# Memory attention of the prompt in split fp32r operands: three one-pass matmuls in place of each two-pass fp32 matmul

## The chip, the cores and the metric

The kernel runs on one core of one Trainium2 chip. Its time is the device time of one execution in microseconds (us). A profile is one execution recorded by the hardware profiler. TensorE is PE in the rows (PEld its weight loads), VectorE is DVE, ScalarE is ACT, GpSimd is POOL, and SP issues nearly all DMAs, in order.

## What is computed

A decoder step of two layers over 512 prompt tokens and 8 x 8 sample tokens. Each layer ends with cross-attention into 256 memory tokens (four heads of 256) and a gated feed-forward network. The cross-attention, from the reference:

```python
def mem_attend(h, k, v, w_q, w_o):
    B, T, _ = h.shape
    q = (h @ w_q).reshape(B, T, MEM_HEADS, MEM_HEAD_DIM)
    s = jnp.einsum('bthe,bnhe->bhtn', q, k, preferred_element_type=F32) * MEM_HEAD_DIM ** -0.5
    p = jax.nn.softmax(s, axis=-1)
    o = jnp.einsum('bhtn,bnhe->bthe', p, v.astype(F32)).reshape(B, T, D_MODEL).astype(h.dtype)
    return o @ w_o
```

For the prompt, k and v are projected from the memory tokens in the kernel; for the sample they are read from a cache, 256 KB for each sequence, head and side.

## The kernel before

Activations stand transposed, channels on partitions and the 576 tokens along the columns, in two halves: 256 prompt tokens, and 256 prompt tokens with the 64 of the sample. A projection (`dense`) takes a weight of 128x1024 (`wr`), splits it on ScalarE into a high part in fp32r (`wh`, a cast) and on VectorE into the rest (`wl`, a subtraction), and makes each product of three one-pass matmuls: high by high, high by rest, rest by high. A matmul of plain fp32 operands runs in two passes, and the trace has two records for it.

A memory-attention stage (`mem_stage`, once in each layer) is written out by `sched`, a scheduler that works with fixed numbers at build time: every generator yields how much TensorE work it has just issued and how long to stay away, and the scheduler picks who issues next. Its filler is the projection of Q. Its lanes are two chains of `mem_prompt` (one for each half, four heads each), one chain of `mem_sample` (four heads, two blocks of four sequences), and the output projection, which waits for heads that are done.

- `mem_prompt(l, h, hf, ...)`: four matmuls for the scores of 256 tokens with 256 memory tokens; maximum on VectorE; exponential on ScalarE; division on VectorE; four transposes of the probabilities on TensorE, a copy on ScalarE; four matmuls with V; then the result is split into `oh` and `ol` for the output projection.
- `mem_sample(l, h, blk, ...)`: takes four K loads from the stream, eight small matmuls for the scores (32x256 in the rows), softmax, two transposes, takes four V loads, eight matmuls with V.

The loads of the sample's K and V come from `_Stream`. It issues a load into columns that the arena gives out, at the place in the program where `get` or `fill` is called; it loads ahead, up to eight, only while there is room:

```python
    def fill(self, n):
        while self.srcs and len(self.q) < n and self.prog.room() >= self.reserve + 512:
            self.load()
...
        return TOTAL - self.G * sum(int(p.taken.sum()) if p.dt == F32 else len(p.taken) for p in self.pages
                                    if p.taken.any())
```

The second piece is the arena's `room`: of 41472 columns it takes off the used ones of fp32 pages, and whole pages where they hold fp32r. The reserve here is `MROOM`, 4500. A load waits on SP until the last reader of its columns is done, and every DMA behind it on SP waits with it. All engines' instructions are recorded at one line (L630), so tiles tell them apart: `page` is the arena, `in_cmk` and `in_cmv` are the cached K and V, `in_w` the weights, `p` PSUM.

Of the kernel before, what the change touches and what calls it, by code (L numbers as in the profile page):

```python
# [9 lines left out]
F32R = mybir.dt.float32r  # L10
# [691 lines left out]
class _Prog:  # L702
# [1188 lines left out]
    def mem_stage(self, l, nx):  # L1891
        nc = self.nc
        Q = self.wide("mq", dt=F32)
        oh, ol = self.wide("xh"), self.wide("xl")
        done = set()

        def ev(i, hf, ps):
            t0, N = HALF[hf]
            nx.upto(hf)
            nc.vector.tensor_tensor(Q[i][:, t0:t0 + N], ps[:, :N], nx.R[:, t0:t0 + N], op=OP.mult)  # L1900
            done.add((i, hf))
            if len(done) == 2 * KT:
                nx.clear()

        q = lambda: self.dense(self.pos[f"mq{l}"], 8, KT, nx.h, nx.l, ev, first=6)

        fin = set()
        st = _Stream(self, [s for h in range(4) for k in range(2) for s in self.mem_src(l, h, k)], "Kb", 8, MROOM)
        lanes = [self.chain(*[self.mem_prompt(l, h, hf, Q, done, oh, ol, fin) for h in range(4)]) for hf in range(2)]
        lanes.append(self.chain(*[self.mem_sample(l, h, b, Q, done, st, oh, ol, fin) for h in range(4) for b in range(2)]))  # L1910
        nn = _Next(self, "g_ffn", l * 8)
        ready = lambda k: lambda: sum((k // 2, j) in fin for j in ("a0", "a1", "s0", "s1")) == 4

        def o():
            yield 0, 0, lambda: len(done) == 2 * KT
            yield from self.dense(self.pos[f"mo{l}"], 8, KT, oh, ol, self.res_evac(nn), first=6, ready=ready)

        f = self.sched(lanes + [o()], q(), METM)
        assert f is None or next(f, None) is None
        self.Kc[l], self.Vc[l] = None, None  # L1920
        return nn
# [2 lines left out]
        b = range(blk * 4, blk * 4 + 4)  # L1924
        return [self.aps["cmk"][l, i, h] for i in b] + [self.aps["cmv"][l, i, h] for i in b]

    def mem_prompt(self, l, h, hf, Q, done, oh, ol, fin):
        nc = self.nc
        yield 0, 0, lambda: (2 * h, hf) in done and (2 * h + 1, hf) in done and self.Vc.get(l) is not None and len(self.Vc[l]) == 4
        K, V = self.Kc[l], self.Vc[l]  # L1930
        mx, den = self.T([128, 2], "mx"), self.T([128, 2], "den")
        ps = self.PS()
        for tt in range(2):
            t = slice(hf * 256 + tt * 128, hf * 256 + tt * 128 + 128)
            for eh in range(2):
                nc.tensor.matmul(ps[:, tt * 256:tt * 256 + 256], Q[2 * h + eh][:, t], K[h][:, eh * 256:eh * 256 + 256],
                                 start=eh == 0, stop=eh == 1)
        nc.vector.tensor_reduce(mx[:], ps[:].rearrange("p (h n) -> p h n", h=2), axis=AX.X, op=OP.max)
        nc.vector.tensor_scalar(mx[:], mx[:], -1.0 / 16, None, op0=OP.mult)
        yield 1.7, 1.2  # L1940
        p_ = self.S([128, 512], s="P")
        for tt in range(2):
            c = slice(tt * 256, tt * 256 + 256)
            nc.scalar.activation(p_[:, c], ps[:, c], AF.Exp, bias=mx[:, tt:tt + 1], scale=1.0 / 16,
                                 accum_out=den[:, tt:tt + 1])
        del ps
        yield 0, 1.2
        nc.vector.reciprocal(den[:], den[:])
        for tt in range(2):
            c = slice(tt * 256, tt * 256 + 256)  # L1950
            nc.vector.tensor_scalar(p_[:, c], p_[:, c], den[:, tt:tt + 1], None, op0=OP.mult)
        yield 0, 1.2
        ps = self.PS()
        for tt in range(2):
            for kt in range(2):
                nc.tensor.transpose(ps[:, kt * 256 + tt * 128:kt * 256 + tt * 128 + 128],
                                    p_[:, tt * 256 + kt * 128:tt * 256 + kt * 128 + 128], self.ident)
        pt = self.S([128, 512], s="PT")
        nc.scalar.copy(pt[:], ps[:])
        del p_  # L1960
        yield 0.44, 1.5
        ps = self.PS()
        for vh in range(2):
            for kt in range(2):
                c = (h % 2) * 256 + vh * 128
                nc.tensor.matmul(ps[:, vh * 256:vh * 256 + 256], V[kt, h // 2][:, c:c + 128],
                                 pt[:, kt * 256:kt * 256 + 256], start=kt == 0, stop=kt == 1)
        d = slice(hf * 256, hf * 256 + 256)
        for vh in range(2):
            self.split(ps[:, vh * 256:vh * 256 + 256], oh[2 * h + vh][:, d], ol[2 * h + vh][:, d])  # L1970
        fin.add((h, f"a{hf}"))
        yield 1.7, 0

    def mem_sample(self, l, h, blk, Q, done, st, oh, ol, fin):

# [529 lines left out]
```

## Time and profile before

| | us |
|---|---|
| three runs: median (lowest to highest) | 2044.92 (2040.68 to 2045.32) |
| the profiled execution: its time | 2044.57 |
| its span, first to last instruction | 2042.4 |
| PE busy, share of the span | 1987.4, 97% |
| DVE, ACT, POOL busy | 1252.5, 798.2, 264.2 |
| stage of layer 0: from 398 to 563, PE busy | 162.19 of 165 |
| stage of layer 1: from 1428 to 1592, PE busy | 159.97 of 164 |

Busy time is the time in which an engine had an instruction under way. Matmuls are pipelined, so a matmul's own length is more than its share of the engine; what a matmul costs is read from the start of one row to the start of the next. "Idle before" tells how long an engine stood still ahead of a row, and the name behind the arrow what ended it.

### The profile page before, as it was taken

What the parts mean: (1) busy time and instruction counts of PE and PEld (TensorE: products, weight loads), DVE (VectorE), ACT (ScalarE), POOL (GpSimd) and SP (SyncE); (2) the same over time, 40 slices, a digit from 0 to 9 for tenths busy, and PEclk for the clock granted to TensorE, in tenths of its full rate; (3) what the DMA queues carried; (4) which work ended last, traced back from release to release, by engine and by line L of the source; (5) the groups of instructions that cost most, each with busy time, mean ns of one, the idle gap of its engine ahead of it and who ended that gap; (6) DMA issues with size and microseconds to landing.
All of it is one profiled execution on the core that took longest, in us unless ns stands there. A gap on an engine that the chain in (4) does not pass through costs nothing.

```text
span 2042.4 us, 40671 instructions
## 1 busy us (share of the span) xinstructions
PE 1987.4 (97%) x16443; PEld 1849.4 (91%) x16443; DVE 1252.5 (61%) x3020; ACT 798.2 (39%) x1674; POOL 264.2 (13%) x570
## 2 busy tenths in 40 slices
PE   6999999999999999999999999999999999999997
PEld 6899877978999999999899888879779999999996
DVE  7686676644577467467516676656545675575575
ACT  5564424333444234234322442455334442342342
POOL 1133121000012012011003222200000021121111
PEclk9999999999999999999999999999999999999998
DMA  4221235555322222222554565675553222222222
GB/s 149 73 66 52 76 114 191 169 188 193 108 66 91 84 82 83 83 83 78 167 165 157 196 203 177 220 246 175 171 196 109 80 83 94 74 83 90 76 72 76
DMA packets 104091, 252.29 MB, mean 124 GB/s; under 512 B 11168, under 2 KB 22048, under 8 KB 103904
## 3 DMA queue, kind: packets, MB, share of 16 engines
q1 hardware_dynamic: 103760, 249.49, 37.8%
q8 instruction: 129, 2.11, 0.4%
q14 instruction: 58, 0.48, 0.1%
q10 hardware_dynamic: 144, 0.22, 0.0%
HBM read 227.70 MB, written 21.96 MB: 122 GB/s over the span
## 4 chain that ended last, share of the span: by engine, by line
PE 87%; DVE 6%; ACT 3%; DMA 3%; issue 1%; POOL 0%; SPq 0%; DVEq 0%; ACTq 0%; POOLq 0%
PE p L630 87%; DVE page L630 4%; ACT page L630 2%; DVE wl L630 1%; DMA wr<-in_w 1%; ACT wh L630 1%; DVE rn L630 1%; DMA page<-in_cmk 1%; DMA out_o_ss<-page 0%; DMA page<-xd 0%; DMA page<-in_x 0%; POOL page L630 0%; ACT L630 0%; SPq L630 0%; DMA xd<-page 0%
## 5 line engine op out<-in xcount | busy, mean ns | idle before, releaser
L630 PE MATMUL p<-page,wh 128*128 128x256 f32 (+1 forms) x7296 | 1101.9, 299 | 18.0 <-ACT wh L630 12.8
L630 PEld LDWEIGHTS p<-page,wh 128*128 128x128 f32 x7296 | 1013.2, 191 | 51.2 <-issue 25.8
L630 PE MATMUL p<-page,wl 128*128 128x256 f32 (+1 forms) x3648 | 589.8, 298 | 0.0
L630 PEld LDWEIGHTS p<-page,wl 128*128 128x128 f32 x3648 | 519.8, 191 | 8.2 <-issue 7.2
L630 DVE TENSOR_TENSOR page<-p,page 128x256 f32<-128x256 f32 (+5 forms) x647 | 241.8, 392 | 322.1 <-PE p L630 235.5
L630 ACT CAST wh<-wr 128x1024 fp32r<-128x1024 f32 (+1 forms) x268 | 274.6, 1028 | 378.2 <-PE p L630 297.4
L630 DVE TENSOR_TENSOR wl<-wr,wh 128x1024 fp32r<-128x1024 f32 (+1 forms) x268 | 332.9, 1245 | 83.2 <-ACT wh L630 76.4
L630 DVE SCALAR_TENSOR_TENSOR page<-page,vecs,page 128x256 f32<-128x256 f32 (+4 forms) x545 | 283.8, 526 | 97.5 <-ACT page L630 86.6
L630 PE MATMUL p<-page,page 64*64 64x64 f32 (+13 forms) x3768 | 280.7, 297 | 10.6 <-DVE page L630 4.0
L630 ACT ACTIVATE page<-page,vecs 128x256 f32<-128x256 f32 (+5 forms) x319 | 168.6, 537 | 231.9 <-DVE page L630 226.0
L630 PEld LDWEIGHTS p<-page,page 64*64 64x64 f32 (+6 forms) x3768 | 184.0, 130 | 69.5 <-issue 20.7
L630 POOL COPY page<-page 128x16 f32<-128x16 f32 (+5 forms) x312 | 128.5, 436 | 732.4 <-DVE page L630 732.4
L630 ACT ACTIVATE page<-page 128x256 f32<-128x256 f32 (+6 forms) x293 | 115.8, 410 | 139.1 <-DVE page L630 132.8
L630 POOL TENSOR_TENSOR page<-page,page 128x320 f32<-128x320 f32 (+6 forms) x96 | 91.7, 963 | 446.1 <-DVE page L630 321.8
L630 ACT COPY page<-p 128x256 f32<-128x256 f32 (+8 forms) x161 | 62.5, 413 | 162.4 <-PE p L630 159.9
L630 PE MATMUL p<-wh,page 128*128 128x512 f32 (+1 forms) x368 | 119.1, 397 | 0.0
L630 DVE TENSOR_TENSOR page<-page,page 128x256 fp32r<-128x256 f32 (+8 forms) x181 | 81.5, 463 | 57.4 <-ACT page L630 56.4
L630 DVE TENSOR_TENSOR page<-page 128x256 f32<-128x256 f32 (+5 forms) x222 | 97.9, 454 | 14.6 <-POOL page L630 9.4
L630 ACT CAST page<-page 128x256 fp32r<-128x256 f32 (+2 forms) x118 | 50.1, 439 | 126.0 <-DVE page L630 126.0
L630 PEld LDWEIGHTS p<-wh,page 128*128 128x128 f32 (+1 forms) x368 | 77.3, 223 | 14.5 <-issue 2.5
L630 PE MATMUL p<-cid,page 128*128 128x128 f32 (+3 forms) x669 | 78.3, 258 | 5.6 <-ACT page L630 4.0
L630 POOL MEMSET page<- 128x2 f32 (+4 forms) x110 | 12.2, 111 | 530.6 <-PE p L630 281.8
(84 smaller groups left out, 808.3 us busy)
## 6 DMA issues: line engine op xcount, KB each, us to landing
wr<-in_w SPq DMA_DIRECT2D x252, 512.0 KB, 3.6
page<-in_ck SPq DMA_DIRECT2D x72, 256.0 KB, 5.1
page<-in_cv SPq DMA_DIRECT2D x72, 256.0 KB, 4.4
page<-in_cmk SPq DMA_DIRECT2D x64, 256.0 KB, 5.0
page<-in_cmv SPq DMA_DIRECT2D x64, 256.0 KB, 4.8
wr<-in_w SPq DMA_DIRECT2D x16, 384.0 KB, 3.1
xd<-page SPq DMA_DIRECT2D x16, 288.0 KB, 4.3
out_o_v<-page SPq DMA_DIRECT2D x12, 256.0 KB, 4.5
```

Of the source, the lines that this page charges most:

```text
L630: return f(*args, **kw)
```

## The change

In `mem_prompt`, K, Q, the transposed probabilities and V are each split into a high part and a rest in fp32r, by `split` (a cast on ScalarE, a subtraction on VectorE), and each two-pass matmul becomes three one-pass ones. Parts of K and V of a head are made once and kept in `parts` until the second half of the prompt has used them; those of Q and of the probabilities are made in each call. A new yield of 1.5 stands between the split of Q and the scores, and two yields that stand for matmul work are 1.44 in place of 1.7. The copy of the transposed probabilities becomes the cast of their split. The whole diff:

```diff
@@ -1904,9 +1904,9 @@
 
         q = lambda: self.dense(self.pos[f"mq{l}"], 8, KT, nx.h, nx.l, ev, first=6)
 
-        fin = set()
+        fin, parts = set(), {}
         st = _Stream(self, [s for h in range(4) for k in range(2) for s in self.mem_src(l, h, k)], "Kb", 8, MROOM)
-        lanes = [self.chain(*[self.mem_prompt(l, h, hf, Q, done, oh, ol, fin) for h in range(4)]) for hf in range(2)]
+        lanes = [self.chain(*[self.mem_prompt(l, h, hf, Q, done, parts, oh, ol, fin) for h in range(4)]) for hf in range(2)]
         lanes.append(self.chain(*[self.mem_sample(l, h, b, Q, done, st, oh, ol, fin) for h in range(4) for b in range(2)]))
         nn = _Next(self, "g_ffn", l * 8)
         ready = lambda k: lambda: sum((k // 2, j) in fin for j in ("a0", "a1", "s0", "s1")) == 4
@@ -1924,20 +1924,37 @@
         b = range(blk * 4, blk * 4 + 4)
         return [self.aps["cmk"][l, i, h] for i in b] + [self.aps["cmv"][l, i, h] for i in b]
 
-    def mem_prompt(self, l, h, hf, Q, done, oh, ol, fin):
+    def mem_prompt(self, l, h, hf, Q, done, parts, oh, ol, fin):
         nc = self.nc
         yield 0, 0, lambda: (2 * h, hf) in done and (2 * h + 1, hf) in done and self.Vc.get(l) is not None and len(self.Vc[l]) == 4
-        K, V = self.Kc[l], self.Vc[l]
+        V = self.Vc[l]
         mx, den = self.T([128, 2], "mx"), self.T([128, 2], "den")
+        two = lambda s: [self.S([128, 512], F32R, s=s) for _ in range(2)]
+        if ("k", h) not in parts:
+            kh, kl = parts["k", h] = two("Kp")
+            self.split(self.Kc[l][h][:], kh[:], kl[:])
+        kh, kl = parts["k", h]
+        qh, ql = two("Qp")
+        for eh in range(2):
+            e = slice(eh * 256, eh * 256 + 256)
+            self.split(Q[2 * h + eh][:, hf * 256:hf * 256 + 256], qh[:, e], ql[:, e])
+        yield 0, 1.5
         ps = self.PS()
         for tt in range(2):
-            t = slice(hf * 256 + tt * 128, hf * 256 + tt * 128 + 128)
             for eh in range(2):
-                nc.tensor.matmul(ps[:, tt * 256:tt * 256 + 256], Q[2 * h + eh][:, t], K[h][:, eh * 256:eh * 256 + 256],
-                                 start=eh == 0, stop=eh == 1)
+                t = slice(eh * 256 + tt * 128, eh * 256 + tt * 128 + 128)
+                k = slice(eh * 256, eh * 256 + 256)
+                o = ps[:, tt * 256:tt * 256 + 256]
+                nc.tensor.matmul(o, qh[:, t], kh[:, k], start=eh == 0, stop=False)
+                nc.tensor.matmul(o, qh[:, t], kl[:, k], start=False, stop=False)
+                nc.tensor.matmul(o, ql[:, t], kh[:, k], start=False, stop=eh == 1)
+        del qh, ql, kh, kl
+        if ("q", h) in parts:
+            del parts["k", h]
+        parts["q", h] = True
         nc.vector.tensor_reduce(mx[:], ps[:].rearrange("p (h n) -> p h n", h=2), axis=AX.X, op=OP.max)
         nc.vector.tensor_scalar(mx[:], mx[:], -1.0 / 16, None, op0=OP.mult)
-        yield 1.7, 1.2
+        yield 1.44, 1.2
         p_ = self.S([128, 512], s="P")
         for tt in range(2):
             c = slice(tt * 256, tt * 256 + 256)
@@ -1955,21 +1972,31 @@
             for kt in range(2):
                 nc.tensor.transpose(ps[:, kt * 256 + tt * 128:kt * 256 + tt * 128 + 128],
                                     p_[:, tt * 256 + kt * 128:tt * 256 + kt * 128 + 128], self.ident)
-        pt = self.S([128, 512], s="PT")
-        nc.scalar.copy(pt[:], ps[:])
-        del p_
+        ph, pl = two("Pp")
+        self.split(ps[:], ph[:], pl[:])
+        del p_, ps
+        if ("v", h) not in parts:
+            vh_, vl_ = parts["v", h] = two("Vp")
+            for kt in range(2):
+                e = slice(kt * 256, kt * 256 + 256)
+                self.split(V[kt, h // 2][:, (h % 2) * 256:(h % 2) * 256 + 256], vh_[:, e], vl_[:, e])
+        vh_, vl_ = parts["v", h]
         yield 0.44, 1.5
         ps = self.PS()
         for vh in range(2):
             for kt in range(2):
-                c = (h % 2) * 256 + vh * 128
-                nc.tensor.matmul(ps[:, vh * 256:vh * 256 + 256], V[kt, h // 2][:, c:c + 128],
-                                 pt[:, kt * 256:kt * 256 + 256], start=kt == 0, stop=kt == 1)
+                c = slice(kt * 256 + vh * 128, kt * 256 + vh * 128 + 128)
+                e = slice(kt * 256, kt * 256 + 256)
+                self.mm3(ps[:, vh * 256:vh * 256 + 256], vh_[:, c], vl_[:, c], ph[:, e], pl[:, e], kt == 0, kt == 1)
+        del vh_, vl_, ph, pl
+        if ("p", h) in parts:
+            del parts["v", h]
+        parts["p", h] = True
         d = slice(hf * 256, hf * 256 + 256)
         for vh in range(2):
             self.split(ps[:, vh * 256:vh * 256 + 256], oh[2 * h + vh][:, d], ol[2 * h + vh][:, d])
         fin.add((h, f"a{hf}"))
-        yield 1.7, 0
+        yield 1.44, 0
 
     def mem_sample(self, l, h, blk, Q, done, st, oh, ol, fin):
 
```

The two kernels' orders are the same outside the two stages, but for the columns that the arena gives out. Inside they differ nearly everywhere. Three places:

SP, the loads at the beginning of the stage in layer 0 (`in_cmk`, `in_cmv` as above; `wr` with `in_w` is a weight), before:

```order
L630 DMA wr_4528<-in_w 128x1024
L630 DMA page_3939<-in_cmk 128x512 x4
L630 DMA page_3939<-in_cmv 128x512 x2
L630 DMA page_4197<-in_cmv 128x512 x2
L630 DMA page_3939<-in_cmk 128x512 x4
L630 DMA page_3939<-in_cmv 128x512 x3
L630 DMA page_4197<-in_cmv 128x512
L630 DMA page_4197<-in_cmk 128x512
L630 DMA wr_4793<-in_w 128x1024
L630 DMA wr_4806<-in_w 128x1024
```

and of the changed kernel:

```order
L630 DMA wr_4528<-in_w 128x1024
L630 DMA page_3939<-in_cmk 128x512 x4
L630 DMA page_3939<-in_cmv 128x512 x4
L630 DMA page_3939<-in_cmk 128x512 x4
L630 DMA wr_4820<-in_w 128x1024
L630 DMA wr_4850<-in_w 128x1024
L630 DMA page_3939<-in_cmv 128x512 x4
L630 DMA page_3939<-in_cmk 128x512 x4
L630 DMA wr_5060<-in_w 128x1024
```

Between the weight 4528 and the next weight there were 17 loads of K and V and there are 12; after that loads come in fours, and the weight 5060 stands between a K and a V.

TensorE, from the sample's first matmuls with V (p_4723, in the other kernel p_4744) to the next block's scores (p_4762, p_4787), before:

```order
L630 MATMUL p_4723<-page_3939,page_4197 32x256 x2
L630 MATMUL p_4723<-page_4197 32x256 x2
L630 MATMUL p_4723<-page_3939,page_4197 32x256 x2
L630 MATMUL p_4723<-page_4197 32x256 x2
L630 MATMUL p_4671<-page_4192,wl_4378 128x256 x4
L630 MATMUL p_4671<-page_4193,wl_4378 128x256
L630 MATMUL p_4738<-page_4197,page_2398 128x256 x4
L630 MATMUL p_4747<-cid,page_4197 128x128 x2
L630 MATMUL p_4762<-page_3939,page_4457 32x256 x8
```

and of the changed kernel:

```order
L630 MATMUL p_4717<-cid,page_3939 128x128 x4
L630 MATMUL p_4674<-page_4192,wl_4378 128x256 x4
L630 MATMUL p_4674<-page_4193,wl_4378 128x256 x4
L630 MATMUL p_4744<-page_3939,page_2398 32x256 x8
L630 MATMUL p_4754<-page_4609 128x256 x12
L630 MATMUL p_4774<-cid,page_3939 128x128 x2
L630 MATMUL p_4787<-page_3939,page_4457 32x256 x8
```

The prompt's four matmuls with V (p_4738) are twelve (p_4754). The sample's V loads went into two pages, and both blocks' loads now come from one page, page_3939.

VectorE, ahead of the rest of the weight that is loaded to wr_4793 (wr_4820), at the scores of head 1, before:

```order
L630 TENSOR_TENSOR page_4461<-p_4893,page_4459 128x256 x2
L630 TENSOR_TENSOR page_4457<-p_4884,page_3939 128x320
L630 TENSOR_REDUCE mx_4919<-p_4921 128x2
L630 TENSOR_SCALAR mx_4919<-mx_4919 128x2
L630 TENSOR_REDUCE mx_4928<-p_4935 128x1
L630 TENSOR_SCALAR mx_4928<-mx_4928 128x1
L630 TENSOR_TENSOR wl_4882<-wr_4793,wh_4881 128x1024
```

and of the changed kernel:

```order
L630 TENSOR_TENSOR page_4609<-p_4946,page_4609 128x512
L630 TENSOR_TENSOR page_4609<-page_2398,page_4609 128x256 x2
L630 TENSOR_TENSOR page_4461<-p_4969,page_4459 128x256 x2
L630 TENSOR_TENSOR page_4457<-p_4937,page_3939 128x320
L630 TENSOR_TENSOR page_4609<-page_4457,page_4609 128x256 x2
L630 TENSOR_REDUCE mx_4997<-p_5003 128x1
L630 TENSOR_SCALAR mx_4997<-mx_4997 128x1
L630 TENSOR_TENSOR wl_4935<-wr_4820,wh_4934 128x1024
```

Between the eviction of Q (128x320) and the maximum of the sample's scores (mx, 128x1) stood the prompt's own maximum; now the two subtractions of Q's split stand there.

## Rows read from the trace of the kernel before

**Rows 1.** the page: busy time, then the chain that ended last, by engine
```profile
PE 1987.4 (97%) x16443; PEld 1849.4 (91%) x16443; DVE 1252.5 (61%) x3020; ACT 798.2 (39%) x1674; POOL 264.2 (13%) x570
...
PE 87%; DVE 6%; ACT 3%; DMA 3%; issue 1%; POOL 0%; SPq 0%; DVEq 0%; ACTq 0%; POOLq 0%
```
**Rows 2.** busy time by stretch, the two stages of memory attention
```profile
398.00:563.00 165.00, 162.19 (x1223) 140.59 (x1222) 81.09 (x221) 59.50 (x152) 0.00 (x0) 1.00 0.46 156
1428.00:1592.00 164.00, 159.97 (x1208) 138.12 (x1207) 81.46 (x220) 59.65 (x150) 0.00 (x0) 1.00 0.46 155
```
**Rows 3.** groups by form on PE, 398 to 563 us
```profile
L630 PE MATMUL p<-page,page 128*128 128x256 f32 x128 | 32.5, 386 | 1.6 <-DVE page L630 1.3
```
**Rows 4.** timeline of PE from 427 us: start, length, operation
```profile
427.93 1.89 PE L630 MATMUL p<-page,page 128*128 128x256 f32 x8
429.65 0.38 PE L630 MATMUL p<-cid,page 128*128 128x128 f32 x2
429.97 1.07 PE L630 MATMUL p<-page,page 128*32 128x256 f32 x16
...
435.99 0.48 PE L630 MATMUL p<-page,page 128*128 128x256 f32 x1 [0.87 <-DVE page L630]
```
**Rows 5.** timeline of all engines, 451 to 461 us
```profile
450.70 0.83 PE L630 MATMUL p<-page,page 128*32 128x256 f32 x12
...
453.41 0.33 SPq L630 DMA_DIRECT2D wr<-in_w  x1
...
453.84 1.32 SPq L630 DMA_DIRECT2D page<-in_cmk  x3
...
459.03 2.25 PE L630 MATMUL p<-page,page 128*32 128x256 f32 x15
...
459.77 0.14 PEld L630 LDWEIGHTS p<-page,page 128*32 128x32 f32 x2 [0.60 <-DMA page<-in_cmk]
...
460.43 0.57 PEld L630 LDWEIGHTS p<-page,page 128*32 128x32 f32 x10 [0.53 <-DMA page<-in_cmk]
```
**Rows 6.** the chain that ended last, 398 to 563 us
```profile
454.74 5.65 DMA page<-in_cmk
```
**Rows 7.** timeline of PE in layer 1, 1489 to 1493 us
```profile
1491.80 1.05 PE L630 MATMUL p<-page,page 128*32 128x256 f32 x10 [0.92 <-DMA page<-in_cmk]
```
**Rows 8.** timeline of PE in the output projection, 523 to 533 us
```profile
526.32 2.08 PE L630 MATMUL p<-page,wh 128*128 128x256 f32 x16
528.24 1.12 PE L630 MATMUL p<-page,wl 128*128 128x256 f32 x8
```
**Rows 9.** groups by form on ACT, 398 to 563 us
```profile
L630 ACT CAST page<-p 128x256 fp32r<-128x256 f32 x16 | 6.0, 373 | 17.7 <-PE p L630 13.7 <-DVE page L630 3.9
...
L630 ACT COPY page<-p 128x512 f32<-128x512 f32 x8 | 4.7, 587 | 13.8 <-PE p L630 12.3 <-DMA page<-in_cmv 1.5
```
**Rows 10.** groups by form on DVE, 398 to 563 us
```profile
L630 DVE TENSOR_TENSOR wl<-wr,wh 128x1024 fp32r<-128x1024 f32 x16 | 19.5, 1219 | 2.2 <-ACT wh L630 2.2
...
L630 DVE TENSOR_TENSOR page<-p,page 128x256 fp32r<-128x256 f32 x16 | 6.8, 425 | 25.4 <-ACT page L630 25.4
```
**Rows 11.** timeline of PE, 417 to 421 us
```profile
417.19 3.31 PE L630 MATMUL p<-page,page 128*128 128x256 f32 x24
```
**Rows 12.** timeline of SP, 418 to 442 us
```profile
420.54 1.75 SPq L630 DMA_DIRECT2D page<-in_cmk  x4
```
**Rows 13.** tile in_cmk on SP, 420.4 to 422.1 us: those four loads
```profile
DMA to landing us min/median/max: 2.7/3.5/4.7
```
**Rows 14.** tile in_cmv on SP, 427.2 to 428 us: two loads
```profile
DMA to landing us min/median/max: 2.7/2.8/3.0
```
**Rows 15.** timeline of PE, 87 to 96 us
```profile
91.59 0.48 PE L630 MATMUL p<-cid,page 128*128 128x128 f32 x1 [3.24 <-ACT page L630]
```
**Rows 16.** busy time by stretch, after that wait
```profile
92.00:95.00 3.00, 3.00 (x17) 3.00 (x16) 2.93 (x7) 1.98 (x4) 2.37 (x6) 0.56 0.10 12
```

## The prediction, written before the changed kernel ran

> **What bounds the kernel now.** I began with the page: TensorE is busy for 97% of the span and carries 87% of the chain that ended last [rows 1], so what leaves its order shortens the span, unless TensorE then waits. The change touches only the two memory-attention stages, so next I read the busy time by stretch: in the 165 and 164 us that hold them TensorE idles 2.8 and 4.0 us, at the full 2.4 GHz, with VectorE busy for half of the time and ScalarE for 36% [rows 2]. The reader is to see that almost nothing is left to win from waits here, and much to lose. By form, the two-pass matmuls are 128 records in a stage, two for each of 64 [rows 3].
>
> Third, the timelines. In front of the prompt's scores TensorE waits for the eviction of Q, 0.87 us at the worst place [rows 4]. The sample's loads of K and V are early nearly everywhere, but not by much: at 450.70 + 0.83 = 451.53 a sample's scores end and free three loads' columns, which the next block needs at 459.03. SP first issues a weight's load, which VectorE holds back until 453.41, then the three, and TensorE's weight loads idle 0.60 and 0.53 us for them [rows 5]; the chain runs through the last of these loads, issued 454.74, 5.65 us [rows 6]. In layer 1 the same place costs 0.92 us [rows 7]. So 7.5 us from free to needed is already just too short behind a weight. That decides this change.
>
> **Matmuls.** Four two-pass matmuls take 1.72 us from their start to the next row's (427.93 to 429.65) [rows 4]. Sixteen one-pass ones of the same size take 1.92 us (526.32 to 528.24), 0.12 each [rows 8]; twelve take 1.44. A call has two such groups, there are 16 calls: 32 x 0.28 = **9.0 us less**. Both prices have rows, so the bounds are narrow (8 to 10).
>
> **Splits.** A stage gains on ScalarE 4 casts of 128x512 (K) and 24 of 128x256 (Q 16, V 8), while 8 copies become casts: by the eviction's 0.37 and the copy's 0.59 us, 11 us [rows 9]. VectorE gains 12 subtractions of 512 columns and 24 of 256: by 0.42, and half the weight's 1.22 for 512, 17 us [rows 10]. Both have room. What counts is the chain in front of TensorE: eviction, cast, subtraction, cast, subtraction of Q is about 1.7 us, against some 1.7 us of other matmuls now put between; K or V adds 0.6. I estimate waits of 0.5 us at some ten places a stage, while the eviction waits of before go: **+3 us**, bounds -5 (all waits of before gone) and +10.
>
> **Loads.** This is the large term. The split parts need room in the arena's fp32r pages, a used one of which counts whole, and the stream loads ahead only while 5012 columns are free. The order shows the result: before, 17 loads stand ahead of the weight's load on SP, now 12; until head 3 each four is written just ahead of its matmuls, into columns that the block before frees. SP can run ahead of TensorE only until it meets such a column, and whatever stands behind it on SP waits too. The weights among it are cast some 15 us of TensorE's work after their place in the order, so they don't bind; behind TensorE's own wait for a load stands everything, the projections too. So each load's fate is a distance, from the last use of its columns to the first use of the new data, which I counted along TensorE's new order with the rows' durations (0.12 a one-pass matmul, 1.0 for a sample's eight, whose sixteen records span 1.07 [rows 4]), against a need:
> - four at once: matmuls end at 420.50, the first issue is at 420.54 and the four take 1.75 us [rows 11, 12]; they land 2.7 to 4.7 us after their issues [rows 13]: **6.1 us**; three, 4.9.
> - one or two: two land 2.7 and 3.0 us after their issues [rows 14]; with the same 0.04, and 0.43 between issues, **2.8 and 3.45 us**.
> - behind a weight: scores end 451.53, third lands 454.74 + 5.65 = 460.39 [rows 5, 6], 8.9; a fourth 9.4; the split of Q, now ahead on VectorE, adds up to 1 us: **9.4 to 10.4**, I take 9.9.
>
> Distance, need and wait, layer 0 (layer 1 in brackets, where columns fall otherwise):
> - V, head 0, first block: 1.3 (1.2), one (two): 1.5 (2.2)
> - K, head 0, second block: 2.1 (2.0), two (four): 1.3 (4.1)
> - V, head 0, second block: 6.1, behind a weight whose rest waits less: 4.3 (4.3)
> - V, heads 1 and 2, first block: 5.4, behind a weight: 4.5 each (4.5 each)
> - K, head 1, second block: 2.1 (2.0), two (three): 1.3 (2.9)
> - K, head 2, second block: 1.9, four: 4.2 (4.2)
>
> The other fours have 4.7 us with two late columns, or over 9, and head 3 has room again (five and seven loads stand ahead): no wait. Sum 21.6 and 26.7: **+48 us**. The lower bound takes the two-load need, and 6.1 in place of the weight's, everywhere: 16. The upper adds a microsecond at the six places behind a weight, and one at the first K of heads 1 and 2: 58.
>
> The Trainium skill, DMA: Bandwidth & Descriptors (Anatomy of one DMA), fits a transfer, there one that GpSimd issues, with about 2.0 us plus its bytes over 436 GB/s; for 256 KB that is an estimate of 2.6 us. The trace agrees for the first of a group (2.7) and not for the fourth (4.7). By that formula the loads would cost near the lower bound, an estimate of +20 us in place of +48; the rows are kept.
>
> **Clock.** TensorE waited once 3.24 us early in the kernel [rows 15]; over the 3 us after it the granted clock averaged 0.56, so most of them ran at 1.2 GHz and not at 2.4 [rows 16], while the stages with their 0.9 us waits stand at 1.00 [rows 2]. Nine of my waits exceed 3.24. If each is followed by such 3 us and a little more, it loses 1.5: 13 us; a slower TensorE also lengthens two of the short distances that follow. I take **+9**, bounds 0 and 25 (two such stretches each).
>
> The Trainium skill, TensorE: Matmul & The Clock Gate (HAM oscillation), describes such a kernel: each wait for a DMA sent the engine back to half rate, in every tile. By it alone this term would be the 13.
>
> **Sum**, against the profiled run's 2044.57 (span 2042.4 and 2.2 around it; the median of the runs is 2044.92): 2044.6 - 9.0 + 3 + 48 + 9 = **2095 us**. Outside the two stages the orders of all engines are unchanged, so I add nothing there.
>
> **Rivals.**
> - Loads cost near their lower bound: the waits overlap, since one wait gives SP time to refill for the next. 2044.6 - 9 + 3 + 16 to 2044.6 - 9 + 3 + 23: 2055 to 2062. For it: two loads land in 3 us [rows 14]; against it: the waits of rows 5 and 7 at 7.5 us. 10%.
> - Not slower: the loads stay hidden, because the columns come free earlier than I count. Then only matmuls and eviction waits change: 2044.6 - 9 - 5 to + 3, 2031 to 2039. It decides at a distance of about 6 us for a four on a free queue; seven of the sixteen fours in a stage are under it or behind a weight, and a landing under 2.7 us has no row here. 3%. Between this and the first rival, no measurable change, 4%.
> - The clock stays low through the stages: the nine waits each with two such stretches, and loads at their upper bound: 2044.6 - 9 + 10 + 58 + 25 = 2129. For it: 3.24 us was enough once; against it: the stretches between waits are dense. 6%.
> - My sum, with its terms inside their bounds, 2062 to 2122: 77%.
>
> **How the numbers follow.** A measurement tells about 0.3%, 6 us, from no change: 2038.8 to 2051.1. Faster 3%, same 4%, slower 93%. The range is 2055 to 2122: it takes in the first rival, and leaves out 13%, the high one and those at no change or below. My own sum's 2062 is loads of 26, clock and splits of 0; its 2122 is loads of 58, clock of 20 and splits of 8.
>
> **What would show it.** In the changed profile: 384 one-pass matmul records in the two stages in place of 256 two-pass ones, busy about 9 us less at equal clock; TensorE idle by loads of K and V about 24 us a stage, at seven places, most at the first V of heads 1 and 2; SP issuing fours within 0.1 us of a block's end; the clock below 1.00 behind waits over 3 us; the remainder of the kernel unchanged. Wrong would be: idle of TensorE put down to VectorE or ScalarE above 10 us (then the splits are the price), or loads of K and V issued early in spite of the order.

## The result, and the profile after

The changed kernel takes 2093.18 us (median of 4 runs, 2087.51 to 2096.57); the kernel before, run beside it on the same chip, 2044.12. The ratio is 1.024, 95% interval 1.0211 to 1.0269: 49 us slower. The profiled execution took 2087.51 us, with a span of 2085.7.

The page of the changed kernel, busy time and chain by engine, where before has [rows 1]:
```profile
PE 2004.8 (96%) x16571; PEld 1854.9 (89%) x16571; DVE 1284.4 (62%) x3092; ACT 819.4 (39%) x1730; POOL 265.0 (13%) x570
...
PE 85%; DVE 5%; DMA 5%; ACT 3%; issue 1%; SPq 0%; POOL 0%; DVEq 0%; ACTq 0%; POOLq 0%
```
DMA's share of the chain has gone from 3% to 5%, 2% of the span is 42 us. TensorE's busy time has risen by 17 us although its work is less: records include waits, as will be seen, and some ran at the low clock. The two stages by stretch, where before has [rows 2], then short stretches in them (columns: stretch, its length, busy time of PE, PEld, DVE, ACT, POOL with counts, granted clock, share of the DMA engines, GB/s):
```profile
395.00:582.00 187.00, 170.47 (x1285) 144.27 (x1285) 96.26 (x255) 69.79 (x179) 0.00 (x0) 0.97 0.42 138
1428.00:1613.00 185.00, 165.80 (x1246) 138.51 (x1245) 98.36 (x261) 73.50 (x186) 0.00 (x0) 0.98 0.43 142
...
432.70:436.10 3.40, 0.77 (x5) 0.26 (x3) 2.34 (x7) 1.12 (x3) 0.00 (x0) 1.00 0.96 333
436.20:439.60 3.40, 3.40 (x16) 1.29 (x16) 0.00 (x0) 0.09 (x1) 0.00 (x0) 0.50 0.12 45
490.80:494.20 3.40, 3.29 (x15) 0.98 (x13) 0.00 (x0) 0.00 (x0) 0.00 (x0) 0.50 0.21 79
521.60:524.90 3.30, 3.19 (x17) 1.82 (x17) 1.12 (x3) 0.45 (x2) 0.00 (x0) 0.50 1.03 381
1494.40:1497.70 3.30, 3.30 (x15) 1.07 (x14) 0.00 (x0) 0.00 (x0) 0.00 (x0) 0.50 0.22 81
1579.70:1583.00 3.30, 3.04 (x13) 0.98 (x14) 0.13 (x1) 0.00 (x0) 0.00 (x0) 0.50 1.02 352
```
Five stretches of 3.41 us at 1.2 GHz, none in these stages before. The prompt's matmuls by form on PE, 395 to 582 us; before has [rows 3]:
```profile
L630 PE MATMUL p<-page 128*128 128x256 f32 x176 | 25.1, 288 | 0.0
...
L630 PE MATMUL p<-page,page 128*128 128x256 f32 x16 | 2.7, 281 | 0.0
```
192 records a stage in place of 128, busy 27.8 us in place of 32.5. Timeline of SP at three places of layer 0 (426 to 463 us, then 495 to 530):
```profile
430.52 0.33 SPq L630 DMA_DIRECT2D wr<-in_w  x1
430.94 2.32 SPq L630 DMA_DIRECT2D page<-in_cmv  x4
...
453.92 0.33 SPq L630 DMA_DIRECT2D wr<-in_w  x1
454.29 1.85 SPq L630 DMA_DIRECT2D page<-in_cmv  x4
...
515.82 1.75 SPq L630 DMA_DIRECT2D page<-in_cmk  x4
```
and of PE where these loads are used:
```profile
435.71 5.48 PE L630 MATMUL p<-page 128*32 128x256 f32 x28 [2.63 <-DMA page<-in_cmv]
...
456.50 0.64 PE L630 MATMUL p<-page,wh 128*128 128x256 f32 x4
458.22 1.92 PE L630 MATMUL p<-page,page 128*32 128x256 f32 x6 [1.07 <-DMA page<-in_cmv]
460.40 1.05 PE L630 MATMUL p<-page,page 128*32 128x256 f32 x10 [0.27 <-DMA page<-in_cmv]
461.38 0.51 PE L630 MATMUL p<-page,wh 128*128 128x256 f32 x2
...
518.67 1.26 PE L630 MATMUL p<-page,page 128*32 128x256 f32 x4 [2.16 <-DMA page<-in_cmk]
521.05 2.65 PE L630 MATMUL p<-page,page 128*32 128x256 f32 x12 [1.12 <-DMA page<-in_cmk]
```
Before, SP had three loads of K behind the weight of 453.41 [rows 5], since V was already there; now the whole four of V goes out behind the weight of 453.92, 0.37 us after it. And the idle in brackets is not the whole wait. Sixteen such records span 1.07 us where nothing waits [rows 4]; here they take 3.16 from 458.22 to 461.38, because the four loads land one behind the other, from 458.08 to 460.36, and the records wait for each inside the group. By the view of waits in layer 0, PE waited 7.1 us for in_cmv and 5.2 for in_cmk; from start to start, below, it is twice that.

### The profile page after: what moved, and what is told of

Its sections match the earlier page's. It is cut to its first block, busy times and chain, and to the rows that moved or that the text cites. A ratio compares the mean times of both kernels' runs of the same rounds, so it can differ in the third digit from the quotient of the medians.

```text
span 2085.7 us, 41112 instructions
## 1 busy us (share of the span) xinstructions
PE 2004.8 (96%) x16571; PEld 1854.9 (89%) x16571; DVE 1284.4 (62%) x3092; ACT 819.4 (39%) x1730; POOL 265.0 (13%) x570
## 4 chain that ended last, share of the span: by engine, by line
PE 85%; DVE 5%; DMA 5%; ACT 3%; issue 1%; SPq 0%; POOL 0%; DVEq 0%; ACTq 0%; POOLq 0%
PE p L630 85%; DVE page L630 3%; ACT page L630 2%; DMA page<-in_cmv 2%; DMA page<-in_cmk 1%; DMA wr<-in_w 1%; DVE wl L630 1%; ACT wh L630 1%; SPq L630 0%; DVE rn L630 0%; DMA out_o_ss<-page 0%; DMA page<-xd 0%; DMA page<-in_x 0%; POOL page L630 0%; DMA xd<-page 0%
## 5 line engine op out<-in xcount | busy, mean ns | idle before, releaser
L630 PE MATMUL p<-page,wh 128*128 128x256 f32 (+1 forms) x7296 | 1101.2, 299 | 17.7 <-ACT wh L630 12.5
L630 PEld LDWEIGHTS p<-page,wh 128*128 128x128 f32 x7296 | 1013.1, 191 | 47.8 <-issue 21.3
L630 PE MATMUL p<-page,wl 128*128 128x256 f32 (+1 forms) x3648 | 588.1, 298 | 0.0
L630 PEld LDWEIGHTS p<-page,wl 128*128 128x128 f32 x3648 | 519.4, 191 | 6.5 <-issue 5.5
L630 DVE TENSOR_TENSOR page<-p,page 128x256 f32<-128x256 f32 (+6 forms) x663 | 253.1, 399 | 317.7 <-PE p L630 232.7
L630 ACT CAST wh<-wr 128x1024 fp32r<-128x1024 f32 (+1 forms) x268 | 274.7, 1028 | 370.8 <-PE p L630 296.9
L630 DVE TENSOR_TENSOR wl<-wr,wh 128x1024 fp32r<-128x1024 f32 (+1 forms) x268 | 333.0, 1245 | 82.8 <-ACT wh L630 82.7
L630 DVE SCALAR_TENSOR_TENSOR page<-page,vecs,page 128x256 f32<-128x256 f32 (+4 forms) x545 | 284.9, 528 | 94.1 <-ACT page L630 86.0
L630 ACT ACTIVATE page<-page,vecs 128x256 f32<-128x256 f32 (+5 forms) x319 | 168.6, 537 | 231.4 <-DVE page L630 227.7
L630 PE MATMUL p<-page,page 64*64 64x64 f32 (+13 forms) x3452 | 232.4, 292 | 27.4 <-DMA page<-in_cmk 12.4
L630 POOL COPY page<-page 128x16 f32<-128x16 f32 (+5 forms) x312 | 128.3, 436 | 728.2 <-DVE page L630 728.2
L630 PEld LDWEIGHTS p<-page,page 64*64 64x64 f32 (+6 forms) x3452 | 142.7, 127 | 86.6 <-DMA page<-in_cmk 22.3
L630 ACT ACTIVATE page<-page 128x256 f32<-128x256 f32 (+6 forms) x293 | 115.8, 410 | 136.6 <-DVE page L630 133.7
L630 DVE TENSOR_TENSOR page<-page,page 128x256 fp32r<-128x256 f32 (+9 forms) x264 | 113.2, 450 | 58.4 <-ACT page L630 56.8
L630 POOL TENSOR_TENSOR page<-page,page 128x320 f32<-128x320 f32 (+6 forms) x96 | 92.6, 972 | 441.5 <-DVE page L630 321.7
L630 ACT CAST page<-page 128x256 fp32r<-128x256 f32 (+4 forms) x174 | 72.8, 439 | 132.8 <-DVE page L630 132.8
L630 PE MATMUL p<-wh,page 128*128 128x512 f32 (+1 forms) x368 | 119.1, 397 | 0.0
L630 ACT COPY page<-p 128x256 f32<-128x256 f32 (+8 forms) x145 | 53.1, 394 | 136.1 <-PE p L630 135.0
L630 PE MATMUL p<-page 128*128 128x256 f32 (+7 forms) x816 | 90.7, 297 | 9.1 <-DMA page<-in_cmv 6.9
L630 DVE TENSOR_TENSOR page<-page 128x256 f32<-128x256 f32 (+5 forms) x195 | 89.2, 469 | 15.2 <-POOL page L630 9.4
L630 PEld LDWEIGHTS p<-page 128*128 128x128 f32 (+4 forms) x816 | 68.0, 156 | 28.1 <-DVE page L630 9.0
L630 PEld LDWEIGHTS p<-wh,page 128*128 128x128 f32 (+1 forms) x368 | 77.3, 223 | 14.4 <-issue 2.5
```

The costliest lines, as they stand in the source:

```text
L630: return f(*args, **kw)
```

## The experiments

All times are medians of the runs of one kernel; each was compared with the kernel before on its own chip. In the rows of some runs the helper's line is L632, L639 or L644 in place of L630, since their edits move it. Two theories of the loss stood at first: columns (loads wait because the columns they go to were just freed; my forecast) and splits (the casts and subtractions hold TensorE). After the second four runs a third theory joined: the place of the loads in SP's order, behind the weights.

**Columns held, nothing split.**
```diff
-            self.split(self.Kc[l][h][:], kh[:], kl[:])
...
-                nc.tensor.matmul(o, qh[:, t], kh[:, k], start=eh == 0, stop=False)
...
+                nc.tensor.matmul(ps[:, tt * 256:tt * 256 + 256], Q[2 * h + eh][:, t],
+                                 self.Kc[l][h][:, eh * 256:eh * 256 + 256], start=eh == 0, stop=eh == 1)
```
(and so for P and V; tiles are given out as in the changed kernel.)

> The changed kernel's tiles for the split parts are given out and held for as long as there, but never written: no casts or subtractions for K, Q, P and V, and the matmuls are two-pass ones on the fp32 operands, as before. By the columns theory (the loads of the sample's K and V come late because the arena has no columns that are long free) this pays what the change pays without its gain: the distances between freed and needed are the changed kernel's or a little shorter, so 45 to 70 us above before, with TensorE idle for loads of K and V at 10 to 15 us a stage or more, and stretches at half clock behind the longest waits. By the splits theory (the casts and subtractions hold TensorE up) there is nothing left to pay: within 6 us of before.

2080.88 us, ratio 1.018 (1.0165 to 1.0195): 37 above before. Below my 45 to 70, but without one split the larger part of the loss is there: the splits are not its main cause. Against the kernel before without loads (2039.24, the next experiment) its loads cost 42 us; those of the changed kernel cost 63. Two things that cost there are absent here: the clock stays at 1.00 in its stages,
```profile
398.00:563.00 165.00, 152.34 (x1086) 124.96 (x1087) 70.45 (x198) 51.80 (x134) 0.00 (x0) 1.00 0.44 145
```
and the first K of head 3, whose place costs 6.7 and 6.4 us in the changed kernel (table below), waits for nothing.

**No loads.** In both kernels, with a class whose `get` gives the prompt's K or V in turn (these kernels leave out the sample's own memory, and the sample waits until the prompt's V is there):
```diff
-        st = _Stream(self, [s for h in range(4) for k in range(2) for s in self.mem_src(l, h, k)], "Kb", 8, MROOM)
+        st = _Held(self, l)
```


> The kernel before, but the sample's memory attention reads the prompt's K and V, which are on the chip, in place of its own, so 128 loads of 256 KB are left out. It shows what the loads cost before the change. Columns theory: the two waits read there, 1.1 and 0.9 us, and little else: 0 to 5 us below before. It is the base line for the next run.

> The changed kernel with the same loads left out (the sample reads the prompt's K and V): the splits, the three matmuls and the columns of the parts all stay. Columns theory: all of the loss is gone, and what remains is matmuls -9 and splits +3 (bounds -5 to +10): 6 us below the kernel before without these loads (14 below to 1 above), and no granted clock under 1.00 in the two stages. Splits theory: it stays 35 to 50 us above it, with TensorE waiting for VectorE and ScalarE in the stages.

2039.24 us (0.9975, 0.9962 to 0.9987) and 2029.95 (0.9934, 0.992 to 0.9949). Without loads the change is a gain of 9.3 us. Loads, and what follows from them, cost 5 us before and 63 after. The view of waits, PE alone, 395 to 566 us, kernel before and then changed kernel, both without loads:
```profile
PE p L639 <- DVE page L639: 2.1, 4, 0.9
PE p L639 <- ACT page L639: 0.4, 1, 0.4
```
```profile
PE p L639 <- DVE page L639: 3.7, 6, 1.1
PE p L639 <- ACT page L639: 2.1, 3, 0.7
```
The splits make TensorE wait 3.3 us more in this stage.

**Old columns, early loads.** The fp32 columns of Q, K and V whose parts stand are slots for loads (`_Slot` hands its columns back when dropped); oldest columns first; a smaller reserve.
```diff
-MROOM = 4500
+MROOM = 500
...
+                    if name == "Kb":
+                        key = (0, int(p.stamp[off:off + k].max()), n, off)
...
-        t = self.prog.S([128, 512], s=self.name)
+        t = _Slot(self, self.slots.pop(0)) if len(self.slots) > 1 else self.prog.S([128, 512], s=self.name)
...
+            st.slots.append(self.Kc[l][h])
...
+            st.slots += [_Cols(Q[i].buf, Q[i].c0, 512) for i in (2 * h, 2 * h + 1)]
...
+                st.slots += [V[0, h // 2], V[1, h // 2]]
```


> The changed kernel with all of its loads and matmuls, but the loads get columns that are free longer: the fp32 columns of Q, K and V, dead once their split parts stand, are used as slots for loads; other columns are taken oldest first; and the reserve is 500 columns in place of 4500. Counted along TensorE's order, no load but the first few has under 8 us between the last reader of its columns and its first use (changed kernel: 1.2 to 6 at seven fours). Columns theory: loads +0 to +8, clock 0, matmuls -9, splits +3: 2039 us, from 2030 to 2048, which would be at or under the kernel before. Splits theory: 2080 or more, as the changed kernel.

2032.63 us, ratio 0.9943 (0.9926 to 0.996): faster than both kernels, 60.5 us below the changed one and within 3 of the one without loads. The clock is back, by stretch:
```profile
398.00:563.00 165.00, 159.96 (x1319) 145.05 (x1320) 99.20 (x271) 71.96 (x180) 0.00 (x0) 1.00 0.48 156
1428.00:1592.00 164.00, 158.96 (x1317) 144.16 (x1316) 98.18 (x267) 70.36 (x177) 0.00 (x0) 1.00 0.47 156
```
TensorE's order is the same in this and the changed kernel, so the starts of the same matmul in both tell where the changed kernel loses. The first V of head 1 as an example; here it runs from
```profile
450.23 0.64 PE L644 MATMUL p<-page,wh 128*128 128x256 f32 x4
...
451.80 0.50 PE L644 MATMUL p<-page,wh 128*128 128x256 f32 x2
```
450.23 to 451.80, 1.57 us, in the changed kernel from 456.50 to 461.38, 4.88: 3.3 lost, 0.4 of it regained at a wait for VectorE right behind. All places, the share of the low clock within them:

| | layer 0: forecast, measured | layer 1: forecast, measured |
|---|---|---|
| V, head 0, first block | 1.5, 1.8 | 2.2, 2.5 |
| K, head 0, second | 1.3, 0.4 | 4.1, 2.1 |
| V, head 0, second (behind a weight) | 4.3, 5.0 | 4.3, 4.5 |
| V, head 1, first (behind a weight) | 4.5, 2.8 | 4.5, 3.0 |
| K, head 1, second | 1.3, 1.4 | 2.9, 2.8 |
| V, head 2, first (behind a weight) | 4.5, 4.7 | 4.5, 3.7 |
| K, head 2, second | 4.2, 3.5 | 4.2, 3.5 |
| K, head 3, first | 0, 6.7 | 0, 6.4 |
| sum | 21.6, 26.2 | 26.7, 28.6 |

Seven places are those of the forecast; the eighth is not.

**Splits made, not used**, without loads: the splits of the changed kernel, two-pass matmuls on the fp32 operands.

> The changed kernel without the sample's loads (it reads the prompt's K and V), every split made as there, but the matmuls are the two-pass ones on the fp32 operands. It takes the sum of the run without loads (9.3 us below its base line) apart: matmuls alone would be this run to that one, splits alone the base line to this one. By my terms: splits +3 (bounds -5 to +10), so 2039 + 3 = 2042 us, and 9 above the changed kernel without loads. If the matmuls gave nothing and the splits cost nothing but came with a gain elsewhere: at 2030.

2046.37 us (1.0013, 1.0003 to 1.0022): 7 above the base line and 16 above the changed kernel without loads, each to some 4 us; I had expected 3 and 9. Here P is copied as well as split, which the changed kernel doesn't need, so 7 is probably more than the splits cost there, and 16 more than the matmuls gain.

**No fresh page for a load.**
```diff
-        if best is None or ((best[0][0] or best[3] > 0) and idle > SPARE):
+        if best is None or ((best[0][0] or best[3] > 0) and idle > SPARE and name != "Kb"):
```


> The changed kernel, but a load of K or V never opens a fresh page while an open one has columns for it. For the miss in head 3: there the changed kernel's loads went to a page that the projection of Q had just released (the last eviction of Q ends at 515.74, the loads are issued at 515.82, TensorE needs them at 516.5) and cost 7.0 and 6.7 us in the two stages, where I had counted a fresh page as free at once. With older columns (9.7, 9.7, 3.5 and 15.2 us between last reader and first use) that wait goes: 12 to 14 us below the changed kernel, 2079 to 2082. If the wait had another cause (SP busy, the weights ahead), it stays: 2093.

2079.25 us, 14 below the changed kernel, as expected. In layer 0 K of head 3 is now issued from 508.72 on, and its place costs 0.2 us in place of 6.7. In the changed kernel the loads came 0.08 us after the end of the last eviction of Q on DVE. SP without the fresh page, then DVE in the changed kernel:
```profile
508.72 7.18 SPq L630 DMA_DIRECT2D page<-in_cmk  x4
```
```profile
515.26 0.48 DVE L630 TENSOR_TENSOR page<-p,page 128x320 f32<-128x320 f32 x1
```
**Early loads, young columns.** The first two pieces of the diff of "old columns" alone.

> The changed kernel with the reserve of 500 columns and oldest columns first, but without the dead columns of Q, K and V as slots: the stream is allowed to load ahead into all that the arena has. Theory that the reserve is the cause (columns are there, and the stream may not use them): the loss is gone, 2030 to 2045. Columns theory (the columns themselves are too few, so what is loaded ahead lands in columns just freed): distances are still 2.0 to 2.5 us at three blocks of K and 5.4 us behind a weight at two of V in each stage; about half of the loss stays: 2071, from 2058 to 2080.

2051.10 us (1.0031, 1.0021 to 1.0041): 42 below the changed kernel, outside my 2058 to 2080. The places are those of the changed kernel, each smaller: at the first V of head 1, SP has one load behind the weight and not four,
```profile
451.67 0.33 SPq L632 DMA_DIRECT2D wr<-in_w  x1
452.10 0.37 SPq L632 DMA_DIRECT2D page<-in_cmv  x1
452.53 5.41 SPq L632 DMA_DIRECT2D page<-in_cmk  x4
```
and the place costs 0.7 us, not 2.8. It is 18.5 above the run with old columns, where all four loads of this V are issued ahead of the weight; so the 18.5 are younger columns and less lead together.

**The kernel before, loads late.**
```diff
-MROOM = 4500
+MROOM = 99999
```


> The kernel before with a reserve that is never met, so that no K or V is loaded ahead: each four is written just ahead of its matmuls, as in the changed kernel, but the columns are plenty. Theory that the place of issue in SP's order is what costs: as much as in the changed kernel, 2085 to 2105. Columns theory: in layer 0 only the first block of V, the second of K and single loads of two later blocks have under 6 us, in layer 1 almost none; +6 to +24, I take 2056.

2105.77 us (1.0296, 1.0281 to 1.0312): 62 lost without a split and without a column taken. My 2056 was wrong, and with it columns as the only cause. Its SP, 440 to 470 us:
```profile
458.15 0.33 SPq L630 DMA_DIRECT2D wr<-in_w  x1
458.52 1.86 SPq L630 DMA_DIRECT2D page<-in_cmv  x4
466.34 1.75 SPq L630 DMA_DIRECT2D page<-in_cmk  x4
```
The first V of head 1 goes out behind a weight here too, and costs 5.1 us. And where I had counted one late column of four as one late load, it is the first of the four: the K at 466.34 waits for the matmuls of the block before, and the other three, whose columns are free, stand behind it.

**One half of the change.** Scores split alone, or values alone; reserve 6500.

> Half of the change: only the scores (Q and K) are split, the values stay two-pass ones (reserve 6500 in place of 4500; in neither is anything loaded ahead). If the loss is proportional to the split work or to the columns taken, half of it: 2065 to 2072. Columns theory: it is a threshold, since the pages of K and Q alone already leave the loads only columns just freed; the distances are those of the run that only held the columns, 1.2 to 6 us: 2044.6 - 4.5 + 2 + 37 = 2079, from 2070 to 2090.

> The other half: only P and V are split, the scores stay two-pass ones (reserve 6500). If the loss is proportional: 2065 to 2072, and both halves add up to the whole, +49. Columns theory: distances of 2.4 to 3.7 us at the second blocks of K and 4.7 behind a weight at the first blocks of V, so some 17 us of loads a stage: 2044.6 - 4.5 + 2 + 34 = 2076, from 2064 to 2086, and both halves together lose clearly more than the whole.

2099.46 us (1.0272, 1.0252 to 1.0292) and 2087.57 (1.022, 1.0203 to 1.0237): 56 and 44 lost, where both halves together lose 49. Both are above my ranges, but the loss does not grow with the amount of splitting. The raised reserve of 6500 keeps nearly every load of both runs from going out ahead, so they do not show whether half of the columns would have done that at 4500.

**Loads issued by GpSimd**, in the changed kernel and in the kernel before with late loads.
```diff
-        self.prog.nc.sync.dma_start(t[:], self.srcs.pop(0))
+        (self.prog.nc.gpsimd if self.name == "Kb" else self.prog.nc.sync).dma_start(t[:], self.srcs.pop(0))
```


> The changed kernel with one difference: the sample's K and V are issued by GpSimd, idle in the stages, in place of SP, so they no longer stand behind the weights' loads. Weights theory (new, since the kernel before with late loads lost 61 us with columns to spare): at the second V of head 0 and the first V of heads 1 and 2 the loads go out 0.4 us after a weight that VectorE held back, and these places cost 4.8, 2.8 and 4.7 us in layer 0 and 4.5, 2.9 and 3.7 in layer 1, with three of the five stretches at half clock: that comes back, 28 us, 2065, from 2055 to 2075. The waits for columns and for the fresh page in head 3 stay, some 27 us. Columns theory alone: the loads wait for columns and not for the queue, 2085 to 2095. A transfer that GpSimd issues may take another time than one of SP; no row of before shows it.

> The kernel before with nothing loaded ahead (61 us slower), and the K and V issued by GpSimd. Weights theory: the second V of head 0 and the first V of heads 1 to 3, 21 us in layer 0 and 22 in layer 1, and some 10 of clock behind them come back: 2052, from 2045 to 2068. If the loads were late for another reason (columns, or landing times), it stays at 2095 to 2106.

2089.29 us (1.0218, 1.0203 to 1.0233) and 2083.45 (1.0206, 1.0183 to 1.0228): 4 and 22 regained of the 28 and 54 that I expected. The places behind a weight, 23.7 us in the changed kernel, are at 0 in both, measured as above (one at 0.4). But others grew. POOL in the second kernel, 440 to 535 us, and PE where that K is used:
```profile
455.70 0.54 POOL L630 DMA_DIRECT2D page<-in_cmv  x1 [9.10 <-PE p L630]
460.93 2.12 POOL L630 DMA_DIRECT2D page<-in_cmk  x4 [4.69 <-PE p L630]
```
```profile
459.53 1.07 PE L630 MATMUL p<-page,page 128*32 128x256 f32 x16
...
464.62 0.59 PE L630 MATMUL p<-page,page 128*32 128x256 f32 x2 [1.64 <-DMA page<-in_cmk]
```
The sixteen records that free its columns end at 460.6, and TensorE needs K from 463.0 on (464.62 less 1.64), 2.4 us later: with the weight's wait gone, the columns' is longer (K of head 1, second block, costs 4.8, low clock behind it included, in place of 1.4 in the changed kernel's layer 0). Moving the queue alone only hands the wait on. In the changed kernel it also came with low clock for 44 us of the two stages in place of 17, and with 6.3 us lost at the start of the first, most of it in a wait for VectorE ahead of all uses of the loads. DVE and PE there, then PE in the run that splits the scores alone:
```profile
384.50 0.89 DVE L630 TENSOR_TENSOR page<-p,page 128x320 f32<-128x320 f32 x2 [5.45 <-DMA page<-xd]
...
402.07 2.08 PE L630 MATMUL p<-page,cid 128*128 128x256 f32 x4 [4.01 <-DVE page L630]
```
```profile
401.01 2.08 PE L630 MATMUL p<-page,cid 128*128 128x256 f32 x4 [2.92 <-DVE page L630]
```
VectorE does these evictions 5 us later than in the changed kernel (379.51), behind a load of `xd`, which is read before the stage, and does not idle from there on. The run with the scores alone, whose loads SP issues, has a like wait, so GpSimd's queue is not needed for it; why the load of `xd` lands later is open.

## Why the prediction was right, point by point

- **Sum.** 2095 us forecast, 2093.18 measured, in the range. That it came so close is partly luck: the loads were too cheap at one place and too dear at others, and the clock came out right by other stretches than I had counted.
- **Matmuls**, -9.0: two stages of 32.5 - 27.8 = 4.7 us less busy, 9.4 in all. Right. A fp32 matmul, two records, takes 0.43 us from start to start (1.72 for four [rows 4]), as much as 3.6 one-pass ones of 0.12; that is why three of those are cheaper than the "two passes", of which the trace shows the two records alone.
- **Splits**, +3, bounds -5 to +10: 3.3 us in the one stage shown, so about 6, and under the 7 of the run that made them idle. Inside the bounds, twice the value. Matmuls and splits together are -9.3 by the medians without loads (their intervals leave 4 us either way), against -6.
- **Loads**, +48, and **Clock**, +9: 57 forecast. From start to start 54.8 us were lost against the run with old columns. (Both are profiled runs; the changed kernel's was its fastest, and by the medians the two kernels are 60.5 apart, so some 5 us stand in no trace.) Five stretches of 3.41 us at half the clock cost at most 1.7 each, 8.5, which leaves 46. The clock term has the right size for another reason: I had nine stretches of 1.5 behind waits of over 3.24 us [rows 15]; there were five, beside idles of 1.94 to 2.63.
- **The step that failed** is "head 3 has room again ... no wait". 13 of the 55 us are lost there. A page that no load had used before was counted as free, but it was a page that the projection of Q still held until 515.74; the run without fresh pages gives 14 us back. Against it the seven places of my table cost 41.6 with the clock in it, where I had 48 without: the first V of head 1 (2.8 and 3.0, not 4.5), the second K of head 0, and the four at the second K of head 2 were oversized. The second V of head 0 cost 5.0 and 4.5, near my 4.3; but with a distance of 6.1 that 4.3 needs 10.4, the upper end, while I wrote that its weight waits less.
- **The reason** was half of it. The weights ahead of a load stood in my sum, as a longer need at three places a stage, 26.6 in all, where 23.7 were measured. But I counted every distance from the last use of the load's columns, as if a load into old columns could not be late; the kernel before with late loads, columns to spare, lost 62. The runs show three releasers of a load that is written at its use, and the last one counts: the last reader of its columns (18 us of the 55), the weight ahead of it on SP (24), the page (13). Against the kernel before, in us:

| | changed kernel, young columns | changed kernel, old columns | kernel before |
|---|---|---|---|
| loads written at their use | +49 | not run | +62 |
| loads written ahead | +7 | -12 | 0 |

So what the change took away is above all the lead in SP's order: 42 us come back with a smaller reserve and oldest columns first, and 18.5 more with the dead columns. That the lead went because room went is shown by the run that only held the columns. How the three releasers share the 55 us is read place by place; moving the loads to GpSimd shows that taking one away lets another count.
- **What would show it:** 192 records a stage, fours issued right at a release, clock at 0.97 and 0.98, loads 26 and 29 us a stage (24 forecast): as written. Not as written: the view of waits shows only half of that as idle, the places are eight, and the most is lost at the first K of head 3, not at the first V of heads 1 and 2. Idle put down to VectorE and ScalarE, by the view of waits, is 9.5 us in the two stages, under the 10 that would have spoken for the splits.
- The Trainium skill, TensorE: Matmul & The Clock Gate (HAM oscillation), tells of a kernel whose clock fell at every wait for a DMA. Here it fell at 5 of 16 such places. By that rule alone, as an estimate, the clock would have cost up to 16 times 1.7, 27 us.
- The Trainium skill, DMA: Bandwidth & Descriptors (Anatomy of one DMA), gives an estimate of 2.6 us for 256 KB issued by GpSimd; a lone one took 2.8 here (455.70), those of a four 3.6 to 4.2 (460.93). As on SP, it holds for a load alone, and +20 for the loads, the sum by it, was far from 46.

## What to carry to other kernels

Ask of every change that takes SBUF what stops being loaded ahead. A load written at its use is released by the latest of three: its columns' last reader, whatever stands ahead on its queue, and the release of its page; a count of one alone misjudges it, and one young column at the head of a group holds the group. Operands whose split copies stand are dead columns: given to the loads, along with a smaller reserve and oldest columns first, they turned a loss of 49 us into a gain of 12.

## What the runs showed of the hardware

A TensorE record under way can be a wait: sixteen small matmuls took 3.16 us in place of 1.07, with only 1.34 in brackets, so idle by the view of waits is half of what the loads cost. SP issued 0.04 us after a release and 0.44 apart; GpSimd 0.3 after, and 0.53 apart. In the stages of the changed kernel, 3.41 us at 1.2 GHz lay beside five of its six idles of 1.94 to 2.63 us, shorter than the 3.24 from which I had priced the clock.
